# Instance normalisation on one core: all normalisation on VectorE, and the last tile in two pieces

## The chip, the cores and the metric

The kernel runs on one core of one Trainium2 chip. The metric is the device time of one execution in microseconds (us), lower is better. A single-core run shows one span, whose start and end lie inside the reported time (the kernel before: span 1247.6 us, time 1249.3 us). All runs told of here count as fast runs, at a granted clock of 1.0 (the share of full TensorE clock that the profile shows).

The engines are called PE (TensorE), DVE (VectorE), ACT (ScalarE), POOL (GpSimd) and SP (SyncE). "Landing" is the moment when a transfer's completion semaphore reaches its full count.

## The reference

```python
x: (8, 64, 32, 64, 64) float32        # 512 instances of 131072 elements, 268 MB
mean = np.mean(x, axis=(2, 3, 4), keepdims=True)
var  = np.var(x, axis=(2, 3, 4), keepdims=True)
out  = (x - mean) / np.sqrt(var + eps)
```

Every byte comes in once and goes out once: 537 MB in all.

## The kernel before

A tile holds 8 instances on 128 partitions (16 partitions each) and 8192 columns: 4 MB, 64 tiles. Six tile buffers are used in turn. SP issues the loads, ACT issues the stores.

```python
SLOTS = 6
...
def compute(t):
    cut = F // 2                                            # F = 8192
    sums = stat_pool.tile([P, 2], fp32, name="sums")
    nc.vector.reduce_sum(out=sums[:, 0:1], in_=t[:, :cut], axis=mybir.AxisListType.X)
    nc.scalar.activation(out=unused[:, cut:], in_=t[:, cut:], func=Act.Identity,
                         accum_out=sums[:, 1:2])
    mean_ps = ...; nc.tensor.matmul(out=mean_ps, lhsT=avg, rhs=sums, ...)   # sum over the 16 partitions
    nc.vector.tensor_reduce(out=neg_mean, in_=mean_ps, op=Alu.add, negate=True, ...)
    nc.scalar.activation(out=unused, in_=t, func=Act.Square, bias=neg_mean, accum_out=squares)
    var_ps = ...; nc.tensor.matmul(out=var_ps, lhsT=avg, rhs=squares, ...)
    nc.scalar.activation(out=std, in_=var_ps, func=Act.Sqrt, bias=eps_t)
    nc.vector.reciprocal(out=scale, in_=std)
    nc.vector.tensor_mul(out=bias, in0=neg_mean, in1=scale)
    nc.vector.tensor_scalar(out=t[:, cut:], in0=t[:, cut:], scalar1=scale, scalar2=bias,
                            op0=Alu.mult, op1=Alu.add)      # DVE's half
    nc.scalar.activation(out=t[:, :cut], in_=t[:, :cut], func=Act.Identity,
                         scale=scale, bias=bias)            # ACT's half

with tc.manual_schedule():
    for g in range(n_tiles):
        t = load(g)                                         # nc.sync.dma_start
        compute(t)
        nc.scalar.dma_start(out=out_t[g], in_=t)
```

Of the kernel before, what the change touches and what calls it, by code (L numbers as in the profile page):

```python
# [1 line left out]

# [4 lines left out]


@with_exitstack
def kernel(  # L10
    ctx: ExitStack,
    tc: tile.TileContext,
    x: bass.AP,
    eps: bass.AP,
    out: bass.AP,
):
    nc = tc.nc
    fp32 = mybir.dt.float32
    Alu = mybir.AluOpType
    Act = mybir.ActivationFunctionType  # L20

    P = 128
    B, C, D, H, W = x.shape
    n_inst = B * C
    n_elem = D * H * W
    eps_f = float(eps)

    SPLIT = 16
    IPT = P // SPLIT
    F = n_elem // SPLIT  # L30
    n_tiles = n_inst // IPT
    SLOTS = 6

    x_t = x.rearrange("b c d h w -> (b c) (d h w)").rearrange(
        "(k i) (s f) -> k (i s) f", i=IPT, s=SPLIT
    )
    out_t = out.rearrange("b c d h w -> (b c) (d h w)").rearrange(
        "(k i) (s f) -> k (i s) f", i=IPT, s=SPLIT
    )

    singles = ctx.enter_context(tc.tile_pool(name="singles", bufs=1))
    data_pool = ctx.enter_context(tc.tile_pool(name="data", bufs=SLOTS))
    stat_pool = ctx.enter_context(tc.tile_pool(name="stats", bufs=4))
    psum_pool = ctx.enter_context(
        tc.tile_pool(name="psum", bufs=2, space=bass.MemoryType.PSUM)
    )


    avg = singles.tile([P, P], fp32, name="avg")
    nc.vector.memset(avg, 1.0 / n_elem)  # L50
    nc.gpsimd.affine_select(  # L51
        out=avg,
        in_=avg,
        pattern=[[-SPLIT, IPT], [0, SPLIT]],
        compare_op=Alu.is_ge,
        fill=0.0,
        base=0,
        channel_multiplier=1,
    )
    nc.gpsimd.affine_select(  # L60
        out=avg,
        in_=avg,
        pattern=[[SPLIT, IPT], [0, SPLIT]],
        compare_op=Alu.is_ge,
        fill=0.0,
        base=SPLIT - 1,
        channel_multiplier=-1,
    )

    eps_t = singles.tile([P, 1], fp32, name="eps_t")  # L70
    nc.vector.memset(eps_t, eps_f)  # L71

    unused = singles.tile([P, F], mybir.dt.uint8, name="unused")

    def load(g):
        t = data_pool.tile([P, F], fp32, name="xt")
        nc.sync.dma_start(out=t, in_=x_t[g])
        return t

    def compute(t):  # L80
        cut = F // 2
        sums = stat_pool.tile([P, 2], fp32, name="sums")
        nc.vector.reduce_sum(  # L83
            out=sums[:, 0:1], in_=t[:, :cut], axis=mybir.AxisListType.X
        )
        nc.scalar.activation(  # L86
            out=unused[:, cut:],
            in_=t[:, cut:],
            func=Act.Identity,
            accum_out=sums[:, 1:2],  # L90
        )
        mean_ps = psum_pool.tile([P, 2], fp32, name="mean_ps")
        nc.tensor.matmul(out=mean_ps, lhsT=avg, rhs=sums, start=True, stop=True)  # L93
        neg_mean = stat_pool.tile([P, 1], fp32, name="neg_mean")
        nc.vector.tensor_reduce(  # L95
            out=neg_mean,
            in_=mean_ps,
            axis=mybir.AxisListType.X,
            op=Alu.add,
            negate=True,  # L100
        )
        squares = stat_pool.tile([P, 1], fp32, name="squares")
        nc.scalar.activation(  # L103
            out=unused, in_=t, func=Act.Square, bias=neg_mean, accum_out=squares
        )
        var_ps = psum_pool.tile([P, 1], fp32, name="var_ps")
        nc.tensor.matmul(out=var_ps, lhsT=avg, rhs=squares, start=True, stop=True)  # L107
        std = stat_pool.tile([P, 1], fp32, name="std")
        nc.scalar.activation(out=std, in_=var_ps, func=Act.Sqrt, bias=eps_t)  # L109
        scale = stat_pool.tile([P, 1], fp32, name="scale")  # L110
        nc.vector.reciprocal(out=scale, in_=std)  # L111
        bias = stat_pool.tile([P, 1], fp32, name="bias")
        nc.vector.tensor_mul(out=bias, in0=neg_mean, in1=scale)  # L113
        nc.vector.tensor_scalar(  # L114
            out=t[:, cut:],
            in0=t[:, cut:],
            scalar1=scale,
            scalar2=bias,
            op0=Alu.mult,
            op1=Alu.add,  # L120
        )
        nc.scalar.activation(  # L122
            out=t[:, :cut], in_=t[:, :cut], func=Act.Identity, scale=scale, bias=bias
        )


    with tc.manual_schedule():
        for g in range(n_tiles):
            t = load(g)
            compute(t)  # L130
            nc.scalar.dma_start(out=out_t[g], in_=t)  # L131


# [1 line left out]
_INS = ['x', 'eps']  # L135
_OUTS = [((8, 64, 32, 64, 64), 'float32')]

_NUMBERS = {'eps': 9.999999747378752e-06}


# [26 lines left out]
```

## Time and profile before

1249.3 us (1249.26 to 1250.57 in four runs).

| what | reading |
|---|---|
| DMA engines | 90% busy or more in 39 of 40 slices, 430 GB/s over the span |
| ACT, DVE busy | 961.6 us (77%), 467.4 us (37%) |
| DMA time for a tile in and a tile out | 19.4 us |
| compute chain of a tile when its data is already there | 17.5 us |

The first lines come from the page of the kernel before: the busy share of the DMA engines and the rate in 40 equal slices of the span, then the costliest groups of instructions (line, engine, operation, tiles, shapes, count, busy time in us, mean ns of one, idle time before them and what ended it).

```profile
DMA  9999999999999999999999999999999999999998
GB/s 403 420 437 434 434 427 436 435 435 427 435 436 434 434 428 435 435 434 427 437 435 434 433 429 437 435 432 427 437 436 434 429 431 435 436 434 425 437 436 364
...
L103 ACT ACTIVATE unused<-xt,neg_mean 128x8192 uint8<-128x8192 f32 x64 | 455.8, 7121 | 100.6 <-DVE neg_mean L95 100.6
L83 DVE TENSOR_REDUCE sums<-xt 128x1 f32<-128x4096 f32 x64 | 282.8, 4419 | 167.6 <-DMA xt<-in_x_dram 167.6
L86 ACT ACTIVATE unused<-xt 128x4096 uint8<-128x4096 f32 x64 | 231.5, 3617 | 96.1 <-DMA xt<-in_x_dram 91.5
L122 ACT ACTIVATE xt<-xt,bias,scale 128x4096 f32<-128x4096 f32 x64 | 243.3, 3801 | 31.3 <-DVE bias L113 31.3
...
L114 DVE TENSOR_SCALAR xt<-xt,scale,bias 128x4096 f32<-128x4096 f32 x64 | 154.4, 2413 | 2.7 <-DVE bias L113 0.3
```

The kernel is bound by the transfers: the DMA engines leave no slice free until the last one. Compute has slack (17.5 us of work against 19.4 us of transfer per tile), and DVE and ACT wait for data. The waits of the load queue agree. SP's loads wait for stores to land, because only then is a buffer free:

```profile
SPq L77 <- DMA out_dram<-xt: 1122.4, 58, 43.3
```

Now the end of the timeline before (start in us, duration, engine, line, operation, count, idle time before it and what ended it). ACTq is an instruction of ACT's queue that starts a transfer.

```profile
1151.66 3.80 ACT L122 ACTIVATE xt<-xt,bias,scale 128x4096 f32<-128x4096 f32 x1 [0.48 <-DVE bias L113]
1157.00 4.42 DVE L83 TENSOR_REDUCE sums<-xt 128x1 f32<-128x4096 f32 x1 [2.99 <-DMA xt<-in_x_dram]
1157.08 0.34 ACTq L131 DMA_DIRECT2D out_dram<-xt  x1
...
1233.18 0.34 ACTq L131 DMA_DIRECT2D out_dram<-xt  x1
```

ACT finishes the normalisation of tile 59 at 1151.66 + 3.80 = 1155.46, but its store starts only at 1157.08, just when the data of tile 60 lands.

### The profile page before, as it was taken

How to read it: one execution, taken by the hardware profiler on the slowest of the kernel's cores; microseconds unless marked ns; L12 is line 12 of the kernel's file. 1: busy time of each engine (PE TensorE's matmuls, PEld its weight loads, DVE VectorE, ACT ScalarE, POOL GpSimd, SP SyncE). 2: the span in 40 equal slices, each digit the busy share in tenths (PEclk: the TensorE clock that was granted, in tenths of full speed). 3: DMA queues.
4: the chain of work that ended last, by engine and by line, in shares of the span. 5: the costliest groups of instructions: out<-in, count | busy, mean ns of one | idle time of the engine just before them, and what ended most of it. 6: DMA issues, size and time to landing. Idle time of an engine off the chain costs nothing.

```text
span 1247.6 us, 1828 instructions
## 1 busy us (share of the span) xinstructions
PE 73.6 (6%) x256; PEld 64.2 (5%) x256; DVE 467.4 (37%) x322; ACT 961.6 (77%) x386; POOL 0.9 (0%) x6
## 2 busy tenths in 40 slices
PE   0000000000000000000000000000000000000000
PEld 0000000000000000000000000000000000000000
DVE  2344433433334334343343433434334333343331
ACT  5888888787777877778777777777787777877774
POOL 0000000000000000000000000000000000000000
DMA  9999999999999999999999999999999999999998
GB/s 403 420 437 434 434 427 436 435 435 427 435 436 434 434 428 435 435 434 427 437 435 434 433 429 437 435 432 427 437 436 434 429 431 435 436 434 425 437 436 364
DMA packets 18443, 536.99 MB, mean 430 GB/s; under 512 B 2048, under 2 KB 2048, under 8 KB 2048
## 3 DMA queue, kind: packets, MB, share of 16 engines
q1 hardware_dynamic: 9216, 268.44, 49.9%
q10 hardware_dynamic: 9216, 268.44, 49.8%
q14 instruction: 9, 0.07, 0.0%
q8 instruction: 2, 0.03, 0.0%
HBM read 268.44 MB, written 268.44 MB: 430 GB/s over the span
## 4 chain that ended last, share of the span: by engine, by line
ACT 45%; DVE 32%; another core or an unknown queue 12%; PE 6%; issue 2%; DMA 1%; ACTq 0%
ACT unused L103 37%; DVE sums L83 19%; DVE xt L114 10%; ACT xt L122 4%; ACT unused L86 3%; PE var_ps L107 3%; PE mean_ps L93 3%; ACT std L109 1%; DMA xt<-in_x_dram 1%; DVE scale L111 1%; DVE neg_mean L95 1%; DVE bias L113 1%; ACTq L131 0%; ACT L109 0%
## 5 line engine op out<-in xcount | busy, mean ns | idle before, releaser
L103 ACT ACTIVATE unused<-xt,neg_mean 128x8192 uint8<-128x8192 f32 x64 | 455.8, 7121 | 100.6 <-DVE neg_mean L95 100.6
L83 DVE TENSOR_REDUCE sums<-xt 128x1 f32<-128x4096 f32 x64 | 282.8, 4419 | 167.6 <-DMA xt<-in_x_dram 167.6
L86 ACT ACTIVATE unused<-xt 128x4096 uint8<-128x4096 f32 x64 | 231.5, 3617 | 96.1 <-DMA xt<-in_x_dram 91.5
L122 ACT ACTIVATE xt<-xt,bias,scale 128x4096 f32<-128x4096 f32 x64 | 243.3, 3801 | 31.3 <-DVE bias L113 31.3
L111 DVE RECIPROCAL scale<-std 128x1 f32<-128x1 f32 x64 | 10.5, 164 | 530.8 <-ACT std L109 530.8
L114 DVE TENSOR_SCALAR xt<-xt,scale,bias 128x4096 f32<-128x4096 f32 x64 | 154.4, 2413 | 2.7 <-DVE bias L113 0.3
L93 PE MATMUL mean_ps<-sums,avg 128*128 128x2 f32 x128 | 36.0, 351 | 670.9 <-DVE sums L83 573.9
L93 PEld LDWEIGHTS mean_ps<-sums,avg 128*128 128x128 f32 x128 | 32.1, 311 | 674.7 <-ACT unused L86 657.1
L107 PE MATMUL var_ps<-squares,avg 128*128 128x1 f32 x128 | 37.6, 363 | 484.1 <-ACT unused L103 484.1
L107 PEld LDWEIGHTS var_ps<-squares,avg 128*128 128x128 f32 x128 | 32.1, 312 | 489.6 <-ACT unused L103 489.6
L109 ACT ACTIVATE std<-var_ps,eps_t 128x1 f32<-128x1 f32 x64 | 16.7, 261 | 42.7 <-PE var_ps L107 42.7
L95 DVE TENSOR_REDUCE neg_mean<-mean_ps 128x1 f32<-128x2 f32 x64 | 10.2, 160 | 60.1 <-PE mean_ps L93 60.1
L103 ACT ACTIVATION_READ_ACCUMULATOR unused<-xt,neg_mean 128x1 f32 x64 | 11.9, 187 | 0.0
L86 ACT ACTIVATION_READ_ACCUMULATOR unused<-xt 128x1 f32 x64 | 11.9, 186 | 0.0
L113 DVE TENSOR_TENSOR bias<-neg_mean,scale 128x1 f32<-128x1 f32 x64 | 10.2, 160 | 2.2
L86 ACT ACT_TABLE_LOAD x1 | 1.3, 1283 | 0.8 <-PEq L148 0.8
L109 ACT ACT_TABLE_LOAD x1 | 1.3, 1283 | 0.0
L50 DVE MEMSET avg<- 128x128 f32 x1 | 0.2, 165 | 0.9 <-PEq L148 0.9
L51 POOL TENSOR_SCALAR_AFFINE_SELECT avg<-avg 128x128 f32<-128x128 f32 x1 | 0.3, 343 | 0.6 <-DVE eps_t L71 0.6
L60 POOL TENSOR_SCALAR_AFFINE_SELECT avg<-avg 128x128 f32<-128x128 f32 x1 | 0.3, 338 | 0.1
L148 POOL MEMSET const-bfloat16-1.0<- 128x1 bf16 x1 | 0.1, 102 | 0.0
L148 POOL MEMSET const-uint8-127<- 128x1 uint8 x1 | 0.1, 102 | 0.0
(3 smaller groups left out, 0.3 us busy)
## 6 DMA issues: line engine op xcount, KB each, us to landing
xt<-in_x_dram SPq DMA_DIRECT2D x64, 4096.0 KB, 53.3
out_dram<-xt ACTq DMA_DIRECT2D x64, 4096.0 KB, 45.2
```

The lines of the kernel that those rows point to most:

```text
L51: nc.gpsimd.affine_select(out=avg, in_=avg, pattern=[[-SPLIT, IPT], [0, SPLIT]], compare_op=Alu.is_ge, fill=0.0, base=0, channel_multiplier=1,
L83: nc.vector.reduce_sum(out=sums[:, 0:1], in_=t[:, :cut], axis=mybir.AxisListType.X)
L86: nc.scalar.activation(out=unused[:, cut:], in_=t[:, cut:], func=Act.Identity, accum_out=sums[:, 1:2],)
L93: nc.tensor.matmul(out=mean_ps, lhsT=avg, rhs=sums, start=True, stop=True)
L95: nc.vector.tensor_reduce(out=neg_mean, in_=mean_ps, axis=mybir.AxisListType.X, op=Alu.add, negate=True,)
L103: nc.scalar.activation(out=unused, in_=t, func=Act.Square, bias=neg_mean, accum_out=squares)
L107: nc.tensor.matmul(out=var_ps, lhsT=avg, rhs=squares, start=True, stop=True)
L109: nc.scalar.activation(out=std, in_=var_ps, func=Act.Sqrt, bias=eps_t)
L111: nc.vector.reciprocal(out=scale, in_=std)
L113: nc.vector.tensor_mul(out=bias, in0=neg_mean, in1=scale)
L114: nc.vector.tensor_scalar(out=t[:, cut:], in0=t[:, cut:], scalar1=scale, scalar2=bias, op0=Alu.mult, op1=Alu.add,)
L122: nc.scalar.activation(out=t[:, :cut], in_=t[:, :cut], func=Act.Identity, scale=scale, bias=bias)
```

## The change

The intent is to take ACT's half of the normalisation away, to write it as (x - mean) * scale so that the small bias product goes, to rebalance the first sums, and to cut the last tile in two pieces so that its first half can be stored sooner. The two queues and the six buffers stay as they are. The averaging matrix now carries a minus sign, so that the mean comes out negated. The diff, cut to its core:

```diff
+    FULL = P * COLS // n_elem                                # 8 instances
+    groups = [(i, FULL) for i in range(0, n_inst - FULL, FULL)]
+    tail = [(n_inst - FULL, FULL // 2), (n_inst - FULL // 2, FULL // 2)]
...
-    nc.vector.memset(avg, 1.0 / n_elem)
+        nc.vector.memset(neg, -1.0 / n_elem)                 # one matrix per tile height
...
-        cut = F // 2
+        a = w * 29 // 64                                     # DVE sums 3712 of 8192 columns
...
-        bias = stat_pool.tile([P, 1], fp32, name="bias")
-        nc.vector.tensor_mul(out=bias, in0=neg_mean, in1=scale)
         nc.vector.tensor_scalar(
-            out=t[:, cut:], in0=t[:, cut:], scalar1=scale, scalar2=bias, op0=Alu.mult, op1=Alu.add)
-        nc.scalar.activation(
-            out=t[:, :cut], in_=t[:, :cut], func=Act.Identity, scale=scale, bias=bias)
+            out=t, in0=t, scalar1=neg_mean, scalar2=scale, op0=Alu.add, op1=Alu.mult)
...
+        t = data_pool.tile([P, COLS], fp32, name="xt")       # the last tile
+        half = COLS // 2
+        parts = [t[:, :half], t[:, half:]]
+        for p, (first, n) in zip(parts, tail):
+            load(p, first, n)
+        for p, (first, n) in zip(parts, tail):
+            compute(p, n)
+            store(p, first, n)
```

Each piece holds four instances on 128 partitions, so its rows are 16 KB per partition in place of 32 KB.

More of the change, by code (lines that the diff above doesn't have):

```diff
@@ L26 @@
     eps_f = float(eps)
-    SPLIT = 16
-    IPT = P // SPLIT
-    F = n_elem // SPLIT
-    n_tiles = n_inst // IPT
     SLOTS = 6
-    x_t = x.rearrange("b c d h w -> (b c) (d h w)").rearrange(
-        "(k i) (s f) -> k (i s) f", i=IPT, s=SPLIT
-    )
-    out_t = out.rearrange("b c d h w -> (b c) (d h w)").rearrange(
-        "(k i) (s f) -> k (i s) f", i=IPT, s=SPLIT
-    )
+    COLS = 8192
+    x_f = x.rearrange("b c d h w -> (b c) (d h w)")
+    out_f = out.rearrange("b c d h w -> (b c) (d h w)")
+    FULL = P * COLS // n_elem
+    groups = [(i, FULL) for i in range(0, n_inst - FULL, FULL)]
+    tail = [(n_inst - FULL, FULL // 2), (n_inst - FULL // 2, FULL // 2)]
     singles = ctx.enter_context(tc.tile_pool(name="singles", bufs=1))
@@ L46, with averaging @@
     )
-    avg = singles.tile([P, P], fp32, name="avg")
-    nc.vector.memset(avg, 1.0 / n_elem)
-    nc.gpsimd.affine_select(
-        out=avg,
-        in_=avg,
-        pattern=[[-SPLIT, IPT], [0, SPLIT]],
-        compare_op=Alu.is_ge,
-        fill=0.0,
-        base=0,
-        channel_multiplier=1,
-    )
-    nc.gpsimd.affine_select(
-        out=avg,
-        in_=avg,
-        pattern=[[SPLIT, IPT], [0, SPLIT]],
-        compare_op=Alu.is_ge,
-        fill=0.0,
-        base=SPLIT - 1,
-        channel_multiplier=-1,
-    )
+    def averaging(split):
+        neg = singles.tile([P, P], fp32, name=f"neg{split}")
+        nc.vector.memset(neg, -1.0 / n_elem)
+        nc.gpsimd.affine_select(
+            out=neg,
+            in_=neg,
+            pattern=[[-split, P // split], [0, split]],
+            compare_op=Alu.is_ge,
+            fill=0.0,
+            base=0,
+            channel_multiplier=1,
+        )
+        nc.gpsimd.affine_select(
+            out=neg,
+            in_=neg,
+            pattern=[[split, P // split], [0, split]],
+            compare_op=Alu.is_ge,
+            fill=0.0,
+            base=split - 1,
+            channel_multiplier=-1,
+        )
+        return neg
@@ L70 @@
+    negs = {n: averaging(P // n) for n in sorted({n for _, n in groups + tail})}
     eps_t = singles.tile([P, 1], fp32, name="eps_t")
     nc.vector.memset(eps_t, eps_f)
-    unused = singles.tile([P, F], mybir.dt.uint8, name="unused")
-    def load(g):
-        t = data_pool.tile([P, F], fp32, name="xt")
-        nc.sync.dma_start(out=t, in_=x_t[g])
-        return t
-    def compute(t):
-        cut = F // 2
+    copies = singles.tile([P, COLS - COLS * 29 // 64], mybir.dt.uint8, name="copies")
@@ L82, in compute, with rows, load, store @@
+    powers = singles.tile([P, COLS], mybir.dt.uint8, name="powers")
+    def rows(ap, first, n):
+        return ap[first : first + n].rearrange("i (s f) -> (i s) f", s=P // n)
+    def load(t, first, n):
+        nc.sync.dma_start(out=t, in_=rows(x_f, first, n))
+    def store(t, first, n):
+        nc.scalar.dma_start(out=rows(out_f, first, n), in_=t)
+    def compute(t, n):
+        w = t.shape[1]
+        a = w * 29 // 64
+        neg = negs[n]
         sums = stat_pool.tile([P, 2], fp32, name="sums")
@@ L83, in compute @@
         nc.vector.reduce_sum(
-            out=sums[:, 0:1], in_=t[:, :cut], axis=mybir.AxisListType.X
+            out=sums[:, 0:1], in_=t[:, :a], axis=mybir.AxisListType.X
         )
         nc.scalar.activation(
-            out=unused[:, cut:],
-            in_=t[:, cut:],
+            out=copies[:, : w - a],
+            in_=t[:, a:],
             func=Act.Identity,
@@ L91, in compute @@
         )
-        mean_ps = psum_pool.tile([P, 2], fp32, name="mean_ps")
-        nc.tensor.matmul(out=mean_ps, lhsT=avg, rhs=sums, start=True, stop=True)
+        halves = psum_pool.tile([P, 2], fp32, name="halves")
+        nc.tensor.matmul(out=halves, lhsT=neg, rhs=sums, start=True, stop=True)
         neg_mean = stat_pool.tile([P, 1], fp32, name="neg_mean")
-        nc.vector.tensor_reduce(
-            out=neg_mean,
-            in_=mean_ps,
-            axis=mybir.AxisListType.X,
-            op=Alu.add,
-            negate=True,
-        )
+        nc.vector.reduce_sum(out=neg_mean, in_=halves, axis=mybir.AxisListType.X)
@@ L102, in compute @@
         squares = stat_pool.tile([P, 1], fp32, name="squares")
         nc.scalar.activation(
-            out=unused, in_=t, func=Act.Square, bias=neg_mean, accum_out=squares
-        )
-        var_ps = psum_pool.tile([P, 1], fp32, name="var_ps")
-        nc.tensor.matmul(out=var_ps, lhsT=avg, rhs=squares, start=True, stop=True)
+            out=powers[:, :w],
+            in_=t,
+            func=Act.Square,
+            bias=neg_mean,
+            accum_out=squares,
+        )
+        neg_var = psum_pool.tile([P, 1], fp32, name="neg_var")
@@ L108, in compute @@
+        nc.tensor.matmul(out=neg_var, lhsT=neg, rhs=squares, start=True, stop=True)
         std = stat_pool.tile([P, 1], fp32, name="std")
-        nc.scalar.activation(out=std, in_=var_ps, func=Act.Sqrt, bias=eps_t)
+        nc.scalar.activation(
+            out=std, in_=neg_var, func=Act.Sqrt, scale=-1.0, bias=eps_t
+        )
         scale = stat_pool.tile([P, 1], fp32, name="scale")
         nc.vector.reciprocal(out=scale, in_=std)
-        bias = stat_pool.tile([P, 1], fp32, name="bias")
@@ L113, in compute @@
-        nc.vector.tensor_mul(out=bias, in0=neg_mean, in1=scale)
         nc.vector.tensor_scalar(
-            out=t[:, cut:],
-            in0=t[:, cut:],
-            scalar1=scale,
-            scalar2=bias,
-            op0=Alu.mult,
-            op1=Alu.add,
-        )
-        nc.scalar.activation(
-            out=t[:, :cut], in_=t[:, :cut], func=Act.Identity, scale=scale, bias=bias
+            out=t,
+            in0=t,
+            scalar1=neg_mean,
+            scalar2=scale,
+            op0=Alu.add,
@@ L124, in compute @@
+            op1=Alu.mult,
         )
     with tc.manual_schedule():
-        for g in range(n_tiles):
-            t = load(g)
-            compute(t)
-            nc.scalar.dma_start(out=out_t[g], in_=t)
+        for first, n in groups:
+            t = data_pool.tile([P, COLS], fp32, name="xt")
+            load(t, first, n)
+            compute(t, n)
+            store(t, first, n)
+        t = data_pool.tile([P, COLS], fp32, name="xt")
+        half = COLS // 2
+        parts = [t[:, :half], t[:, half:]]
```

## The prediction

> **What bounds the kernel now.** The DMA engines. The page's DMA row reads 9 (90% or more) in 39 of 40 slices, and the kernel moves 268 MB in and 268 MB out at 430 GB/s over the span. The Trainium skill's page "DMA: Bandwidth & Descriptors", section "Where 436 GB/s comes from", gives 435 GB/s as the ceiling of the 16 ports; this trace's slices read 425 to 437, so it agrees. Estimate from that page: 536.9 MB at 435.2 GB/s is 1233.6 us, so at most 14 of the 1247.6 us of span could ever be saved, and some 5 of these are start and end. The waits of the load queue say the same: SyncE waits 1122 us for stores to land, to get a buffer back.
>
> Per tile the DMA engines need 19.4 us (the interval of the last reductions in the timeline: 1195.85, 1215.31). Compute needs less: while tiles are queued up (start of the timeline) a tile takes 17.5 us from store issue to store issue (31.60, 49.13, 66.62). In the later part both first-pass instructions wait for the load (DVE 167.6 us in 53 waits). The chain of waits names ACT 45% and DVE 32%; that is a chain through compute which itself waits for data, and I don't take it for the bound.
>
> **What the change does.** The load and store queues and the six buffers are as before. Per full tile:
> - Sum split 4096/4096 becomes 3712 (DVE) and 4480 (ACT): DVE 4.42 to about 4.02 us, ACT 3.62 to about 3.95 us.
> - The tiny bias product goes: -0.2 us.
> - ACT's half of the normalisation (3.80 us) goes; DVE's 2.41 us over 4096 columns becomes about 4.65 us over 8192. The skill's "VectorE: DVE Perf Modes", perf-mode tier table, has tensor_scalar at 2x in fp32 and tensor_reduce at 1x; the trace agrees (2.41 against 4.42 us for 4096), and the operation order should not change it.
> - ACT issues the store, so it now waits for DVE's whole normalisation. The chain per tile lengthens by about 0.8 us, 17.5 to about 18.4 us, still below 19.4.
>
> Estimated busy: ACT 962 to about 755 us, DVE 467 to about 580 us. None of it is on the DMA path, so steady state is worth 0.
>
> **The end.** The last load lands at about 1215.2 and its store is issued at 1233.5. Meanwhile earlier stores keep the DMA busy; only the 1232 to 1236 window shows a dip (328 GB/s, about 1 us lost). The two pieces put a half store into the queue about 9 us earlier; ACT works through the pieces in order (about 10 us each), so the last half is issued no earlier, but the queue should not run dry. Worth about -1 us. The second averaging matrix is under 1 us on DVE and POOL, hidden behind the first load (landing at 13.07).
>
> **Prediction: 1248.5 us**, range 1246.3 to 1250.8. Faster by over 2%: 0.01; within 2%: 0.98; slower by over 2%: 0.01.
>
> **What would show it.** DMA row still 9 throughout and about 430 GB/s; ACT near 60%, DVE near 46%; normalisation 4.5 to 4.8 us each, one form for 63 tiles; ACT's idle before the store/next sum up by about 5 us a tile; store interval at the start 18.2 to 18.6 us; fewer tiles that wait for their load (now 53 of 64, then about 40); no dip before the last store.
>
> **What would make it wrong.** Slower: the wide normalisation running at the single rate (about 8.7 us), a tile then taking about 22 us, over the DMA's 19.4: some 1430 us. Or the half-width end transfers running badly, or DVE's traffic slowing the DMA. Faster: the transfer rate being lowered today by ACT's traffic, which I see no sign of.

One reading above is not exact: 37 of the 40 slices read 425 to 437 GB/s, the first two 403 and 420 and the last 364. The highest lies slightly over the page's 435.

## The result, and the profile after

1260.4 us (1259.9 to 1260.57 in four runs) against 1249.3. The ratio is 1.0086, with a 95% interval of 1.0068 to 1.0103. Here and below a ratio is the mean time of one kernel's fast runs over that of the other's of the same rounds, so it is not quite the ratio of the medians quoted. It is slower by 0.9%: inside "within 2%", but outside the predicted range, and the sign is wrong.

The page after, in the same form as before:

```profile
DMA  9999999999999999999999999999999999999986
GB/s 400 432 433 433 433 433 433 433 431 433 433 433 433 432 433 433 433 432 433 433 433 433 433 433 433 433 433 433 433 433 432 433 434 433 433 433 433 428 379 267
...
L107 ACT ACTIVATE powers<-xt,neg_mean 128x8192 uint8<-128x8192 f32 (+1 forms) x65 | 456.1, 7016 | 60.6 <-DVE neg_mean L104 60.6
L95 ACT ACTIVATE copies<-xt 128x4480 uint8<-128x4480 f32 (+1 forms) x65 | 252.1, 3879 | 404.4 <-DMA xt<-in_x_dram 269.8
L122 DVE TENSOR_SCALAR xt<-xt,neg_mean,scale 128x8192 f32<-128x8192 f32 (+1 forms) x65 | 291.2, 4480 | 2.6 <-DVE scale L121 0.3
L92 DVE TENSOR_REDUCE sums<-xt 128x1 f32<-128x3712 f32 (+1 forms) x65 | 257.2, 3957 | 67.0 <-DMA xt<-in_x_dram 67.0
```

Nearly everything is as costed (one full-width normalisation is 4.55 us), and the DMA row is full up to the last two slices: 379 and 267 GB/s, where before only the last slice fell. The loss sits in the last 60 us. The timeline shortly before that:

```profile
1130.93 4.55 DVE L122 TENSOR_SCALAR xt<-xt,neg_mean,scale 128x8192 f32<-128x8192 f32 x1
1136.90 4.02 DVE L92 TENSOR_REDUCE sums<-xt 128x1 f32<-128x3712 f32 x1 [1.43 <-DMA xt<-in_x_dram]
1156.36 0.34 ACTq L85 DMA_DIRECT2D out_dram<-xt  x1
1156.81 3.94 ACT L95 ACTIVATE copies<-xt 128x4480 uint8<-128x4480 f32 x1 [26.11 <-DMA xt<-in_x_dram]
...
1251.61 0.34 ACTq L85 DMA_DIRECT2D out_dram<-xt  x1
```

DVE finished tile 58 at 1130.93 + 4.55 = 1135.48. Its store started at 1156.36, 20.9 us later, and ACT, which issues the stores, did nothing in between. The fourth line needs care: it says that ACT's first pass over tile 59 waited 26.11 us for a load. But tile 59 had landed by 1136.90, when DVE began to reduce it. ACT could not get there, because the store stood in front of it in ACT's queue. It is another load that was waited for.

Which one, the list of compiled instructions tells. This is ACT's part near the end; the names in brackets are the semaphores that each instruction waits for, and DMAHW0 to DMAHW7 are the eight completion semaphores. xt_1183 is tile 58, xt_1202 tile 59, xt_1221 tile 60, xt_1240 tile 61.

```
235 L95 Activation copies_77,sums_1185<-xt_1183 128x4480 [waits DMAHW7_49,Activation_49]
238 L85 DMACopy out_0_dram<-xt_1183 128x8192 [waits DMAHW3_49,DVE_49]
239 L95 Activation copies_77,sums_1204<-xt_1202 128x4480 [waits DMAHW1_49,Activation_49]
242 L85 DMACopy out_0_dram<-xt_1202 128x8192 [waits DMAHW4_49,DVE_49]
243 L95 Activation copies_77,sums_1223<-xt_1221 128x4480 [waits Activation_49]
```

The transfers take the eight semaphores in turn, in the order in which they are scheduled, and a transfer waits until the one that held its semaphore before has landed. In the steady part loads and stores alternate, so loads take the odd turns and stores the even ones, and a store's predecessor is the store four tiles earlier, which is no wait. The loads run six tiles ahead, so at the end only stores are left, and every second one inherits a semaphore from a load:

| order | S57 | L63 | S58 | S59 |
|---|---|---|---|---|
| before: its semaphore was last held by | S53 | L59 | S54 | **L60** |

| order | S57 | L63a | L63b | S58 | S59 |
|---|---|---|---|---|---|
| after: its semaphore was last held by | S53 | L59 | S54 | **L60** | S55 |

(S is a store, L a load, the number the tile.) Before, the store of tile 59 waits for the load one tile ahead, which costs 1.6 us. The split tail adds one load, every later turn moves by one, and the store of tile 58 waits for the load two tiles ahead, with ACT behind it. The landing of that load in the trace (its issue began at 1104.4):

```profile
L82 SPq DMA_DIRECT2D xt<-in_x_dram x1: 328/328/328, 1104.4 to 1104.4; - x1
...
DMA to landing us min/median/max: 51.8/51.8/51.8
```

1104.4 + 51.8 = 1156.2, and the store started at 1156.36.

The Trainium skill, "DMA: Bandwidth & Descriptors", section "Why a DMA increments its semaphore by 16 and not by 1", names a hazard that such a wait excludes: when two DMAs in flight share one semaphore, a wait can pass before the first has fully landed. No run here shows the hazard itself, or that the framework waits because of it. The page asks for one semaphore per in-flight slot. This trace shows the price of sharing eight by turns: 20.9 us of ACT.

What the stall does to the end is seen in windows of 4 us (bounds, length, busy us and count of PE, PEld, DVE, ACT and POOL, granted clock, DMA share, GB/s). First the kernel before, then after:

```profile
1224.00:1228.00 4.00, 0.01 (x1) 0.01 (x1) 0.00 (x0) 3.94 (x2) 0.00 (x0) 1.00 0.95 410
1228.00:1232.00 4.00, 0.58 (x2) 0.49 (x2) 2.73 (x3) 2.91 (x2) 0.00 (x0) 1.00 1.12 483
1232.00:1236.00 4.00, 0.00 (x0) 0.00 (x0) 0.00 (x0) 1.15 (x1) 0.00 (x0) 1.00 0.77 328
```

```profile
1224.00:1228.00 4.00, 0.59 (x2) 0.50 (x2) 3.04 (x2) 0.26 (x1) 0.00 (x0) 1.00 0.04 16
1228.00:1232.00 4.00, 0.00 (x0) 0.00 (x0) 3.67 (x2) 1.85 (x1) 0.00 (x0) 1.00 0.62 262
...
1244.00:1248.00 4.00, 0.00 (x0) 0.00 (x0) 0.10 (x1) 3.80 (x2) 0.00 (x0) 1.00 0.58 244
1248.00:1252.00 4.00, 0.59 (x2) 0.50 (x2) 2.58 (x2) 0.26 (x1) 0.00 (x0) 1.00 0.00 0
```

After the stall ACT takes the remaining tiles back to back, at 18.3 us each, and the stores come out no faster than that. The loads are finished, so the DMA engines have nothing else and run dry.

### The profile page after: what moved, and what is told of

It is laid out like the page before. It is cut to its first block, busy times and chain, and to the rows that moved or that the text cites. A ratio compares the mean times of both kernels' runs of the same rounds, so it can differ in the third digit from the quotient of the medians.

```text
span 1258.9 us, 1715 instructions
## 1 busy us (share of the span) xinstructions
PE 75.4 (6%) x260; PEld 65.2 (5%) x260; DVE 567.6 (45%) x263; ACT 739.8 (59%) x327; POOL 1.4 (0%) x8
## 4 chain that ended last, share of the span: by engine, by line
ACT 59%; DVE 25%; PE 6%; another core or an unknown queue 5%; issue 2%; ACTq 2%; DMA 1%
ACT powers L107 37%; DVE xt L122 23%; ACT copies L95 21%; PE neg_var L115 3%; PE halves L102 3%; ACTq L85 2%; ACT std L117 1%; DMA xt<-in_x_dram 1%; DVE scale L121 1%; DVE neg_mean L104 1%; ACT L117 0%; ACTq L107 0%; ACTq L95 0%
## 5 line engine op out<-in xcount | busy, mean ns | idle before, releaser
L107 ACT ACTIVATE powers<-xt,neg_mean 128x8192 uint8<-128x8192 f32 (+1 forms) x65 | 456.1, 7016 | 60.6 <-DVE neg_mean L104 60.6
L95 ACT ACTIVATE copies<-xt 128x4480 uint8<-128x4480 f32 (+1 forms) x65 | 252.1, 3879 | 404.4 <-DMA xt<-in_x_dram 269.8
L122 DVE TENSOR_SCALAR xt<-xt,neg_mean,scale 128x8192 f32<-128x8192 f32 (+1 forms) x65 | 291.2, 4480 | 2.6 <-DVE scale L121 0.3
L92 DVE TENSOR_REDUCE sums<-xt 128x1 f32<-128x3712 f32 (+1 forms) x65 | 257.2, 3957 | 67.0 <-DMA xt<-in_x_dram 67.0
L102 PE MATMUL halves<-sums,neg 128*128 128x2 f32 x130 | 37.2, 356 | 688.8 <-ACT copies L95 688.8
L102 PEld LDWEIGHTS halves<-sums,neg 128*128 128x128 f32 x130 | 32.6, 311 | 693.3 <-ACT copies L95 676.1
L115 PE MATMUL neg_var<-squares,neg 128*128 128x1 f32 x130 | 38.2, 363 | 484.4 <-ACT powers L107 484.4
L115 PEld LDWEIGHTS neg_var<-squares,neg 128*128 128x128 f32 x130 | 32.6, 312 | 490.0 <-ACT powers L107 490.0
L117 ACT ACTIVATE std<-neg_var,eps_t 128x1 f32<-128x1 f32 x65 | 17.0, 261 | 43.4 <-PE neg_var L115 43.4
L107 ACT ACTIVATION_READ_ACCUMULATOR powers<-xt,neg_mean 128x1 f32 x65 | 12.1, 186 | 0.0
L59 POOL TENSOR_SCALAR_AFFINE_SELECT neg<-neg 128x128 f32<-128x128 f32 x2 | 0.6, 328 | 0.0
```

Of the source, the lines that this page charges most:

```text
L59: nc.gpsimd.affine_select(out=neg, in_=neg, pattern=[[split, P // split], [0, split]], compare_op=Alu.is_ge, fill=0.0, base=split - 1, cha ...
L92: nc.vector.reduce_sum(out=sums[:, 0:1], in_=t[:, :a], axis=mybir.AxisListType.X)
L95: nc.scalar.activation(out=copies[:, : w - a], in_=t[:, a:], func=Act.Identity, accum_out=sums[:, 1:2],)
L102: nc.tensor.matmul(out=halves, lhsT=neg, rhs=sums, start=True, stop=True)
L107: nc.scalar.activation(out=powers[:, :w], in_=t, func=Act.Square, bias=neg_mean, accum_out=squares,)
L115: nc.tensor.matmul(out=neg_var, lhsT=neg, rhs=squares, start=True, stop=True)
```

## The experiments

Three theories at first:

- **Semaphore turn**: the extra load shifts the turns; ACT stands still behind the store of tile 58.
- **Half width**: the two half-width pieces at the end (two chains, 16 KB rows) cost the time.
- **Normalisation**: the longer chain on ACT (18.4 in place of 17.5 us a tile, the store behind DVE) costs it.

Medians of four runs each, with the kernel before run beside them on the same chip:

| run | this, us | before, us | ratio, 95% interval |
|---|---|---|---|
| e1_whole_tail | 1248.41 | 1249.51 | 0.9991 (0.9976 to 1.0006) |
| e2_tiny_load_last | 1262.25 | 1249.51 | 1.0110 (1.0091 to 1.0130) |
| e3_split_one_load | 1253.49 | 1249.51 | 1.0030 (1.0014 to 1.0047) |
| e4_before_split | 1256.97 | 1249.51 | 1.0061 (1.0046 to 1.0076) |
| e5_tiny_load_middle | 1254.52 | 1249.53 | 1.0035 (1.0017 to 1.0053) |
| e6_last_stores_on_sync | 1250.17 | 1249.53 | 1.0014 (0.9989 to 1.0039) |
| e7_first_tile_split | 1250.25 | 1249.53 | 1.0012 (0.9992 to 1.0032) |
| e8_before_tiny_last | 1258.50 | 1249.53 | 1.0070 (1.0055 to 1.0085) |
| e9_last_load_in_half_rows | 1255.70 | 1249.43 | 1.0049 (1.0034 to 1.0064) |
| e10_tiny_load_first | 1248.74 | 1249.43 | 0.9995 (0.9980 to 1.0009) |
| e11_tiny_load_tile_45 | 1250.29 | 1249.43 | 1.0006 (0.9989 to 1.0022) |

The four runs of e1 to e4 shared one chip, as did those of e5 to e8 and those of e9 to e11. On the second chip the times scatter more (e7 from 1248.75 to 1253.35, e6 from 1249.26 to 1256.27).

### e1: the change without the split tail

```diff
-    groups = [(i, FULL) for i in range(0, n_inst - FULL, FULL)]
-    tail = [(n_inst - FULL, FULL // 2), (n_inst - FULL // 2, FULL // 2)]
+    groups = [(i, FULL) for i in range(0, n_inst, FULL)]
+    tail = []
```

> The changed kernel with the last tile in one piece. Semaphore-turn theory (the one extra load shifts the turns of the eight DMA completion semaphores, so the store of tile 58 waits for the load of tile 60): no long wait of ACT before a store, 1248.5 to 1250.0 us. Half-width theory (two half-width chains and transfers at the end cost the 11 us): the same, 1248.5 to 1250. Normalisation theory (the longer ACT chain, 18.4 us a tile with the store behind DVE, costs the 11 us): still about 1260 us.

Measured 1248.41 us. The normalisation theory falls: all of the normalisation on VectorE costs nothing. The stores of tiles 58 and 59 start at 1135.28 and 1156.15, the last one at 1232.28:

```profile
1135.28 0.34 ACTq L85 DMA_DIRECT2D out_dram<-xt  x1
1136.76 3.94 ACT L95 ACTIVATE copies<-xt 128x4480 uint8<-128x4480 f32 x1 [6.29 <-DMA xt<-in_x_dram]
...
1156.15 0.34 ACTq L85 DMA_DIRECT2D out_dram<-xt  x1
...
1232.28 0.34 ACTq L85 DMA_DIRECT2D out_dram<-xt  x1
```

### e2: the same, with 8 KB loaded behind the last tile

```diff
             load(t, first, n)
+            if first == 63 * FULL:
+                nc.sync.dma_start(out=tiny, in_=x_f[0:P, 0:16])
             compute(t, n)
```

> As e1_whole_tail (no split), plus one extra load of 8 KB behind the load of the last tile, read by nobody. Semaphore-turn theory: the store of tile 58 waits about 20 us again for the load of tile 60, stores then follow every 18.4 us (1156, 1175, 1193, 1211, 1230, 1248), and the last full store is issued near 1248 in place of 1233: 1262 to 1265 us. Half-width theory and normalisation theory: 8 KB cost nothing, within 0.5 us of e1_whole_tail.

Measured 1262.25 us: 8 KB that nobody reads cost 13.8 us against e1. No piece is halved here. The stores of tiles 57 and 58:

```profile
1115.56 0.34 ACTq L85 DMA_DIRECT2D out_dram<-xt  x1
...
1155.81 0.34 ACTq L85 DMA_DIRECT2D out_dram<-xt  x1
```

In e1 the same two were issued at 1115.86 and 1135.28. The last store went out at 1247.51, as expected near 1248. In the built program of this run, as in that of the changed kernel, the store of tile 58 waits for the load of tile 60. So the shifted turn causes the loss without any split; that the extra load does not cost by itself is shown by e10.

### e3: the split kept, with one load for both pieces

```diff
-        for p, (first, n) in zip(parts, tail):
-            load(p, first, n)
+        nc.sync.dma_start(
+            out=t.rearrange("p (h f) -> p h f", h=2),
+            in_=x_f[n_inst - FULL : n_inst].rearrange(
+                "(h i) (s f) -> (i s) h f", h=2, s=2 * P // FULL))
```

> The changed kernel with both halves of the last tile fetched by one load (64 loads as before, 65 stores, two half-width chains kept). Semaphore-turn theory: no stall at the store of tile 58, last store at about 1236, 1248 to 1250 us. Half-width theory: half-width chains and half stores are all there, so still about 1260 us (at least 1256).

Measured 1253.49 us, between the two expectations. The stall is gone (store of tile 58 at 1135.42), and 6.9 of the 12.0 us between the changed kernel and e1 go with it. The other 5.1 us were left unexplained. The trace shows that the last load landed late: 62.1 us after its issue in place of 53.2 in e1. That became a new question, taken up in e9.

### e4: the kernel before with the split tail alone

The two pieces, two loads and two stores of the change, put into the kernel before; its normalisation stays shared.

```diff
-        for g in range(n_tiles):
+        for g in range(n_tiles - 1):
...
+        for p, i in parts:
+            nc.sync.dma_start(out=p, in_=x_f[i : i + n].rearrange("i (s f) -> (i s) f", s=P // n))
+        for p, i in parts:
+            compute(p)
+            nc.scalar.dma_start(out=..., in_=p)
```

> The kernel before with only its last tile in two pieces (normalisation shared by ACT and DVE as before). Semaphore-turn theory: the store of tile 58 waits about 20 us to 1157, stores follow every 17.5 us, the last half store is issued near 1247, end 7 us later: 1254 to 1258 us. Normalisation theory: 1248.5 to 1250. Half-width theory: about 1260.

Measured 1256.97 us, with the store of tile 58 at 1158.53 (the store before it at 1118.24) and the last half store at 1249.84. So the loss needs nothing of the new normalisation.

### e5: the extra 8 KB in mid kernel

As e2, with `first == 30 * FULL`.

> As e1_whole_tail, but the unused 8 KB load stands behind the load of tile 30, in mid kernel. Semaphore-turn theory: one store near tile 25 waits some 15 to 20 us for a load two tiles ahead, and ACT stands still as long; but the DMA queues have stores and loads to work off and 30 tiles follow in which ACT (18.4 us a tile) gains about 1 us a tile on the DMA engines (19.4): time within 1 us of e1_whole_tail. If every such stall costs its length: about 11 us over e1_whole_tail.

Measured 1254.52 us (1251.55 to 1255.90): a miss. There was one long wait (the store of tile 25 at 516.11, about 21 us late). In the built program the stores of tiles 26 to 28 also inherit the semaphore of a load two tiles ahead; they followed at 535.45, 554.80 and 574.21, at the pace of the landings. And the DMA rate did not drop then: 421 and 444 GB/s in the two 20 us windows that follow 500. Nor did it cost its length. But it was not free. Loads issued from 400 to 510 landed 53.1 to 53.5 us after their issue; in 1100 to 1125 loads took 56.2 us and stores 43.1, where e1 has 53.2 and 45.0. With more of the queue in loads and less in stores, the last tile landed at 1220.3 (e1: 1214.2), fewer stores were left by then, and the rate fell to 139 and 180 GB/s in 1232 to 1240, before the last store at 1238.31. This reading was tested in e11. (e5 and e1 ran on different chips.)

### e6: the last seven stores issued by SP

```diff
-        for first, n in groups:
+        for first, n in groups[:-5]:          # as before
...                                            # then the loads of the last tiles, and
+        for p, first, n in last:
+            compute(p, n)
+            store(p, first, n, nc.sync)
```

> The changed kernel, split tail and two loads kept, but the last seven stores issued by SyncE behind all loads. The store of tile 58 still waits for the same load, on SyncE, near 1156 to 1163. If the harm is that ACT stands still behind its own store instruction: ACT goes on, the last half store is issued near 1236, 1248 to 1250 us. If the harm is the late store itself, or the half width: about 1260 us.

Measured 1250.17 us, a hair above the expected range, with one run at 1256.27. The split, two loads and half rows are all kept. The stores now wait on SP:

```profile
1136.72 3.94 ACT L95 ACTIVATE copies<-xt 128x4480 uint8<-128x4480 f32 x1 [6.28 <-DMA xt<-in_x_dram]
...
1164.37 66.46 SPq L85 DMA_DIRECT2D out_dram<-xt  x7
```

The first of them goes out at 1164.37, even later than the 1156.36 of the changed kernel, and it does not matter: ACT starts tile 59 at 1136.72 in place of 1156.81, and the DMA engines still move 311 GB/s or more in each 4 us window from 1220 to 1244. So the harm is not the late store; it is that ACT's compute stood behind it.

The run is not a pure test of that, because it also puts the stores behind all loads: the two half loads landed 20.6 and 25.1 us after their issue (57.7 for the second in the changed kernel), at 1184 and 1189, and the last store was issued at 1230.5, earlier than expected. The early landings alone would not have helped the changed kernel: there the last tiles already wait for ACT and not for their loads.

### e7: the split at the first tile

The tile in two pieces (two loads, two chains, two stores) is the first of the kernel; the last is whole.

```diff
-    groups = [(i, FULL) for i in range(0, n_inst - FULL, FULL)]
-    tail = [(n_inst - FULL, FULL // 2), (n_inst - FULL // 2, FULL // 2)]
+    groups = [(i, FULL) for i in range(FULL, n_inst, FULL)]
+    head = [(0, FULL // 2), (FULL // 2, FULL // 2)]        # computed before the others
```

> The changed kernel with the first tile in two pieces (two loads, two stores) and the last whole: 65 loads and 65 stores as in the changed kernel. Semaphore-turn theory: the extra load sits where no store has been issued yet, near the end a store waits only for the load one tile ahead (about 1 us): 1248.5 to 1250.5 us. Half-width theory, in so far as 65 transfers or the narrow forms cost by themselves: above 1252.

Measured 1250.25 us. Sixty-five loads and stores and the half-width forms cost little where they are not at the end: two of the four runs took 1248.75 and 1248.91 us, and the interval includes 1. The scatter of this chip allows no finer statement.

### e8: the kernel before with the 8 KB load at its end

The edit of e2 in the kernel before.

> The kernel before with nothing but the unused 8 KB load added behind the last load. Semaphore-turn theory: the store of tile 58 waits about 20 us, stores then every 17.5 us, the last full store at about 1244.5 in place of 1233.2: 1259 to 1262 us. The others: within 0.5 us of the kernel before.

Measured 1258.50 us, 9.0 above the kernel before (half a microsecond under the expected range), with the store of tile 58 at 1157.29 and the last one at 1244.73. The kernel before has the same weak spot; the place of its turns only hid it.

### e9: the last load in 16 KB rows, everything else whole

What are the 5.1 us of e3? Either the two chains in turn, or the rows of its load. e9 has one full chain and one full store, but a load of two 16 KB rows per partition from two places. Its output is wrong, which doesn't matter for the time.

```diff
+                nc.sync.dma_start(
+                    out=t.rearrange("p (h f) -> p h f", h=2),
+                    in_=x_f[n_inst - 2 * FULL : n_inst].rearrange(
+                        "(h i) (s f) -> (i s) h f", h=2, s=P // FULL)[:, :, : COLS // 2])
```

> As e1_whole_tail (last tile whole, one full-width chain, one full store), but its load comes as two 16 KB rows per partition in one load, from two places that can't be merged; the last 8 instances are wrong on purpose. It asks what the 5 us of e3_split_one_load are. Row theory (while loads and stores compete, a queue with 16 KB rows gets half the share of one with 32 KB rows, so the last load lands about 9 us late and the store backlog is gone before the last store): landing 62 us after issue in place of 53, last store issued near 1241, 1255 to 1259 us. Half-chain theory (two half-width chains in turn cost the 5 us): 1248 to 1249.5.

Measured 1255.70 us, landing 62.1 us after issue, last store at 1241.13: the row theory. The last load, first of e1, then of e9:

```profile
L82 SPq DMA_DIRECT2D xt<-in_x_dram x1: 327/327/327, 1161.0 to 1161.0; - x1
...
DMA to landing us min/median/max: 53.2/53.2/53.2
```

```profile
L138 SPq DMA_DIRECT2D xt<-in_x_dram x1: 388/388/388, 1161.0 to 1161.0; - x1
...
DMA to landing us min/median/max: 62.1/62.1/62.1
```

The queues between 1195 and 1210 us (q1 loads, q10 stores: packets, MB, share of the 16 engines), first of e1, then of e9:

```profile
q1 hardware_dynamic: 107, 3.51, 54.1%
q10 hardware_dynamic: 108, 3.01, 46.6%
```

```profile
q10 hardware_dynamic: 144, 4.19, 64.9%
q1 hardware_dynamic: 141, 2.31, 35.9%
```

In both the two queues move nearly the same number of packets; a packet here is one row, except for 16 small ones (under 512 B) with each transfer. With rows of equal size the queues share the bytes about evenly. With rows half as long the load gets 2.31 MB against 4.19 MB. The Trainium skill, "DMA: Bandwidth & Descriptors", section "Queues, rings and completion order", says that each engine goes round-robin between its queues at packet granularity, typically 9 to 17 descriptors. The trace agrees on round-robin (141 and 144 packets) and shows how long a turn is here: in the packet records of e9 from 1198 to 1204 us, 49 rows of each queue start, in alternating groups of about 16, the number of DMA engines. That is one row a turn.

### e10: the extra 8 KB ahead of everything

```diff
     with tc.manual_schedule():
+        nc.sync.dma_start(out=tiny, in_=x_f[0:P, 0:16])
```

> As e1_whole_tail, with the unused 8 KB load ahead of all others. Semaphore-turn theory: the same extra load that cost 14 us behind the last load costs nothing here, as every turn shifts alike and a store near the end waits only for the load one tile ahead: 1248 to 1250 us, no wait of ACT over 8 us before a store. If an extra load costs by itself: above 1255.

Measured 1248.74 us. The stores of tiles 58 and 59:

```profile
1135.40 0.34 ACTq L85 DMA_DIRECT2D out_dram<-xt  x1
...
1156.25 0.34 ACTq L85 DMA_DIRECT2D out_dram<-xt  x1
```

The same extra load costs 13.8 us at the end and nothing measurable at the start: it is its place among the turns that counts.

### e11: the extra 8 KB behind tile 45

As e5, with `first == 45 * FULL`.

> As e5_tiny_load_middle with the extra load behind the load of tile 45: one wait of about 20 us at the store of tile 40, 23 tiles before the end. Full-recovery theory (as expected before e5): 1248 to 1249.5. Balance theory (the wait is made up by ACT, but leaves fewer stores and more loads in flight for good, so the last load lands later and the DMA engines run dry before the last store): loads land 55 to 58 us after issue from then on, last load landing 4 to 8 us later than in e1_whole_tail, 1251 to 1257 us. No-recovery theory: 1262.

Measured 1250.29 us, between two of the expectations and under the balance theory's 1251. After the wait (store of tile 40 at 806.81, ACT idle for 26.08 us before its next work) loads issued from 888 on took 55.7 to 56.4 us to land, the last tile landed at 1217.6, 3.4 us after e1's 1214.2, and the rate fell to 123 GB/s in 1232 to 1236. The direction is the balance theory's; the size, 1.9 us over e1 (1.6 over e10, which ran on the same chip), is at the low end and small enough that the interval against the kernel before includes 1. Why it is smaller than in e5 stays open (e5 ran on another chip, with more scatter).

## Why the prediction was wrong

- **What bounds the kernel**: right. DMA engines full, steady state unchanged.
- **Costs per tile**: right. The normalisation took 4.55 us (predicted about 4.65), the first sums 4.01 and 3.94 (4.02 and 3.95), stores at the start every 18.4 us (31.64, 50.05, 68.41), ACT busy 740 us (755), DVE 568 (580), 39 of 65 pieces waited for their load (about 40 of 64). The normalisation kept the double rate that the skill's perf-mode tier table gives tensor_scalar in fp32 (4.55 us for 8192 columns, before 2.41 for 4096), in the new order of operations too.
- **"None of it is on the DMA path, so steady state is worth 0"**: right, by e1: the new normalisation with a whole last tile is 1248.41 us, not distinguishable from before.
- **The end, "the last half is issued no earlier, but the queue should not run dry. Worth about -1 us"**: this step failed. It took a store to go out as soon as its tile is normalised. A store also waits for its completion semaphore, and the extra load moved that wait from a load that lands 1.6 us later to one that lands 20.9 us later, with ACT's compute behind it. In place of -1 us the end came 12.2 us later than with a whole last tile, as the sum below shows.

The sum, from the spans and timelines of the changed kernel and e1: the store of tile 58 is 21.1 us later (1156.36 against 1135.28). Four tiles without waiting for loads win back 4.3 us, so the store of tile 62 is 16.8 us later (1229.71 against 1212.88). The two half chains take 21.9 us in place of the 19.4 us from e1's store of tile 62 to its last one, so the last store is 19.3 us later (1251.61 against 1232.28). The end follows 7.3 us after a half store and 14.4 us after a whole one, which gives back 7.1 us. 19.3 - 7.1 = 12.2 us, the difference of the spans (1258.9 and 1246.7).

"The half-width end transfers running badly" stood among the risks. It was real as well, but second: taking the stall away alone left 5.1 us (e3), and e9 shows that 16 KB rows can cause it. In the changed kernel itself this hardly counts, because ACT is late anyway: the second half lands at 1220.6 and is taken up at 1241.1.

The intent of the split had little to win. The Trainium skill, "Perfetto Trace Analysis", section "DMA Optimizations", offers splitting for the case that the DMA engines are generally idle; here they are over 90% busy in all but the last slice.

No version beat the kernel before: e1 is 0.09% faster in the mean, and its interval includes 1. By the prediction's estimate at most 14 us were there to win, and no run here won any of it clear of the noise.

What stays open: that a stall in mid kernel shifts the balance of loads and stores for good is read from e5 and e11, two runs with the same sign and different sizes; no run sets that balance by itself.

## What to carry to other kernels

Where a framework hands out completion semaphores in turn, one more transfer can make a store wait for a load that it has nothing to do with, so look in the compiled list at what each transfer waits for, above all at the end where loads have stopped, and keep such a wait out of the queue of a computing engine. In a trace, compare the end of the last producer with the start of the store: a gap of 1.6 us that ends with somebody else's landing may be a dependency that can grow, and the compiled list tells whether it is. While two queues compete, keep their rows equally long: in e9 the one with rows half as long moved 2.31 MB while the other moved 4.19 MB.

## What the Trainium skill lacked or had wrong

- "DMA: Bandwidth & Descriptors" asks for one semaphore per in-flight slot; neither it nor another page tells what a shared turn costs: the store waits for the former holder, 20.9 us here, and an unread 8 KB load cost 13.8 us (e2) or nothing (e10) by its place alone.
- The same page, section "Queues, rings and completion order", gives the round-robin by packets of typically 9 to 17 descriptors. It doesn't say that a queue's share then goes by its row size: 141 and 144 packets, but 2.31 and 4.19 MB, with rows of 16 and 32 KB (e9).
- "Perfetto Trace Analysis", section "DMA Optimizations", advises splitting only by whether DMA engines are idle. It lacks that the pieces' shorter rows land later beside long ones: 62.1 us in place of 53.2 (e9).
